# Residual tiles of both token halves kept on chip between attention and channel mixer, and the first half's token tiles made inside the second half's output projection

## The chip, the cores and the metric

The kernel runs on one core of one Trainium2 chip, as one program. The metric is the device time of one execution in microseconds (us). Tiles are 128 partitions by 512 float32 columns (256 KB) unless said otherwise.

## The reference

A decoder trunk of two layers over 1024 tokens of width 1024, float32. Layer 0 mixes tokens with two groups of eight heads (dilated window attention and forgetting attention), layer 1 with eight differential heads of value width 128. The parts that the change touches:

```python
for l in range(DEPTH):
    n = rms_norm(h, attn_norm[l])
    h = h + mixer(n)                       # heads, then concat @ w_out
    h = h + conv_glu_ffn(rms_norm(h, ffn_norm[l]), ...)
return rms_norm(h, final_norm)
```

So after the heads of a layer there are an output projection, a residual addition, a normalisation over the width, and a channel mixer (up projection to 2 x 2816, causal convolution over three tokens, SiLU gate, down projection).

## The kernel before

Activations lie transposed: the width on partitions in 8 chunks (index `m`), the tokens in columns, in two halves of 512 (`half` 0 and 1). Every product of two float32 operands is made of three matmuls on a high and a low part (`mm3`, L150; `split`, L162, writes the two parts with one ScalarE copy and one VectorE subtraction).

*Attention and its planner.* A layer's attention is a list of units (32 in layer 0, four for each pair of heads; 16 in layer 1, a head and a token half each). `weave` (L489) merges the units' steps (rows of logits, transposes, products with V, closing steps) with a list of jobs. Each step has a cost and a load; from these the planner makes a goal, the amount of job work that should be done by then, and after every step it runs job generators until the amounts that they yield reach the goal. A job with `after` waits until that unit has ended. TensorE, VectorE and ScalarE then work through queues in a fixed order that the framework's scheduler makes from this order and its own estimates. SP's and POOL's queues issue the DMAs in order: `put` (L193) is SP's, `store` (L196) POOL's.

*The jobs at a layer's end* (`out_jobs`, L1152). The heads' outputs, split, are reloaded or kept in the pool `big` (32 buffers of one tile). `job_out` (L441) then makes the output projection, a chunk `m` and a token half at a time: it asks for the base tile `rt` ahead (`fetch`), multiplies the heads' slices `ks`, and at the end `e` (L1161) adds the base to the sum in PSUM, stores the tile in DRAM (`parts`, seen as `hp` in the trace) and may add its squares to the norm's statistic (`norm_chunk`). In order:

1. heads 0 to 3, both halves, on the layer's input;
2. heads 4 to 7, first half, on the stored tile: the first half is then complete, and its statistic with it;
3. `stats`: the norm factors of the first half;
4. `blocks` (L1174): the eight tiles of the first half are loaded again from DRAM (`t`), scaled by gain and norm factor (`token_blocks`, L1118), stored in DRAM as `half0` (`nt`), and split into `nh` and `nl`, all in one step of the generator;
5. `rest`, heads 4 to 6 of the second half, on the stored tile, 24 steps of three matmuls, stored again.

Head 7 of the second half is left to the channel mixer, as its output comes last.

*Start of the channel mixer* (`channel`, L1323). The attention's buffers are given back, and the channel mixer's pool `fu` opens in their place: 16 buffers `wq`, 8 `sc`, 24 `bt`. `lead(n)` (L1037) runs the next n steps of the up projection: a weight tile is loaded (`wr`, two buffers, on SP), split (L129, L131) and multiplied with the first half's `nh` and `nl`, 12 matmuls a step, and the result goes through `sc` (L931) to DRAM (`e`). Between the leads the second half is finished: eight tiles `x` in `wq` are loaded from `parts` (L1357 to L1359), head 7 is multiplied (tag `dn`), added (L1364), squared and stored again; its statistic and factors follow. Eight tiles of the normalised first half come back from `half0` to `b0`. Then sums and differences of the two halves' blocks are formed (L1378 to L1403) and split by `cut` (L1350) into `bt`, after 24 into `big`: the up projection is a fast product of 2 x 2 blocks in seven products, whose weight sums POOL makes (L824). The down projection loads `parts` again as its residual.

Of the kernel before, what the change touches and what calls it, by code (L numbers as in the profile page):

```python
# [10 lines left out]
F32R = mybir.dt.float32r  # L11
# [7 lines left out]
P = 128  # L19
# [3 lines left out]
HT = 512  # L23
# [10 lines left out]
def f(ap):  # L34
    return ap.bitcast(F32)
# [14 lines left out]
class Trunk:  # L50
# [91 lines left out]
    last = None  # L142
# [47 lines left out]
    def small(self):  # L190
        return self.psp.tile([P, HT], F32, name="small", tag="small")
# [297 lines left out]
    def weave(self, ev, jobs, deadline, margin):  # L489

        ev.sort(key=lambda e: (e[0], e[1]))
        ftotal = sum(j.cost for j in jobs)

        C, L, c, l, first = [], [], 0.0, 0.0, {}
        for k, e in enumerate(ev):
            if e[1] == 0:
                first[e[2]] = k
            c += e[4]  # L500
            l += e[5]
            C.append(c)
            L.append(l)
        pts = [(0, 0.0)]
        for u, nj in sorted(deadline.items()):
            pts.append((first[u - margin], sum(j.cost for j in jobs[:nj])))
        pts.append((len(ev) - 1, ftotal))
        goal = [0.0] * len(ev)
        for (k0, y0), (k1, y1) in zip(pts, pts[1:]):
            dc, dl = C[k1] - C[k0], max(L[k1] - L[k0], 1e-9)  # L510
            for k in range(k0, k1 + 1):
                y = y0 + (y1 - y0 + dc) * (L[k] - L[k0]) / dl - (C[k] - C[k0])
                goal[k] = max(goal[k - 1] if k else 0.0, min(max(y, y0), y1))
        st = {"job": 0, "gen": None, "done": 0.0}
        fins = set()
        lastq = max(k for k, e in enumerate(ev) if e[1] == 1)

        def fill(upto, final=False):
            while st["done"] < upto and st["job"] < len(jobs):
                jb = jobs[st["job"]]  # L520
                if st["gen"] is None:
                    if jb.after is not None and jb.after not in fins and not final:
                        return
                    st["gen"] = jb.gen()
                try:
                    st["done"] += next(st["gen"])
                except StopIteration:
                    st["job"] += 1
                    st["gen"] = None
        for k, (tm, kind, i, fn, cost, load) in enumerate(ev):  # L530
            if kind == 0 and i in deadline:
                while st["job"] < deadline[i]:
                    fill(st["done"] + 0.1)
            if kind in self.pinned and self.last is not None:
                with self.tc.issue_after(getattr(self.last, "ins", self.last)):
                    fn()
            else:
                fn()
            if kind == 6:
                fins.add(i)  # L540
            if k == lastq:
                self.pmap["pj"] = ["A", "D", "A", "D", "D"]
            fill(goal[k])
        fill(1e9, True)
        assert st["job"] == len(jobs), (st["job"], len(jobs))
# [578 lines left out]
    def run(self):  # L1124
# [10 lines left out]
        parts = [[dr.tile([P, T], F32, name=f"hp{l}_{m}") for m in range(8)] for l in range(2)]  # L1135
# [3 lines left out]
        half0 = [dr.tile([P, HT], F32, name=f"nt{m}") for m in range(8)]  # L1139
# [8 lines left out]
        self.odirect = (6, 7)  # L1148
        cs = [slice(hf * HT, (hf + 1) * HT) for hf in range(2)]


        def out_jobs(l, w, base):  # L1152
            st, gi, O = stF[l], 2 * l + 1, Os[l]

            def add(src, norm):
                def b(m, half):
                    t = f(self.big.tile([P, HT], F32R, name="rt", tag="big"))
                    self.store(t, src(m)[:, cs[half]])
                    return t

                def e(m, half, ps, t):  # L1161
                    nc.vector.tensor_tensor(t, t, ps, ALU.add)
                    self.store(parts[l][m][:, cs[half]], t)
                    if norm:
                        self.norm_chunk(st, m, half, t, None)
                return b, e

            def stats():
                self.norm_cols(st, 0)
                yield 0.4  # L1170
                self.norm_rows(st, 0, self.ap, ("rt2", 2))
                yield 0.9

            def blocks():  # L1174
                ts = []
                for m in range(10):
                    if m < 8:
                        t = f(self.big.tile([P, HT], F32R, name="t0", tag="big"))
                        self.put(t, parts[l][m][:, cs[0]])
                        ts.append(t)  # L1180
                    if m == 0:
                        rest.fetch()
                    if 0 < m < 9:
                        self.token_blocks(st, gi, 0, m - 1, ts[m - 1])
                        self.store(half0[m - 1], ts[m - 1])
                    if m > 1:
                        hl = (self.big.tile([P, HT], F32R, name=x, tag="big") for x in ("nh", "nl"))
                        st["h"][m - 2, 0], st["l"][m - 2, 0] = hl
                        self.split(st["h"][m - 2, 0], st["l"][m - 2, 0], ts[m - 2])
                yield 0.0  # L1190
            last = lambda k: 4 * k + 3 if l == 0 else 2 * k + 1
            part = lambda m: parts[l][m]
            jobs = [self.job_load(O, k, last(k)) for k in range(4)]
            jobs += [self.job_out(w, [0, 1, 2, 3], [0, 1], O, *add(base, False), last(3))]
            jobs += [self.job_load(O, k, last(k)) for k in range(4, 6)]
            jobs += [self.job_out(w, [4, 5, 6, 7], [0], O, *add(part, True), 29 if l == 0 else 13)]
            rest = self.job_out(w, [4, 5, 6], [1], O, *add(part, False), 27 if l == 0 else 14, 3)
            jobs += [Job(stats, 1.3), Job(blocks, 0.0)]
            jobs += [rest]
            return jobs  # L1200

        def first_v(src, N):
# [3 lines left out]
        w = a["wqkA"]  # L1206
# [8 lines left out]
        for g in range(2):  # L1215
            w = a["wqkB"]
            J0 += [self.job_v(a["wvB0"], n, 4, 64, (0, 8), True) if g == 0 else
                   self.job_v(a["wvB1"], n, 4, 64, (0, 12))]
            for p in range(2 * g, 2 * g + 2):
                J0 += [self.job_plain(w[2 * p], n, -0.125, qB, p * P),  # L1220
                       self.job_plain(w[2 * p + 1], n, None, kB, p * P)]
        J0 += out_jobs(0, a["woA"], lambda m: a["xT"][m * P:(m + 1) * P, :])
        O0 = "woA7"
        F0 = self.plan_ffn(0)
# [3 lines left out]
        for g in range(4):  # L1228
            w = a["wqkC"]
            if g:  # L1230
                J1 += [self.job_v(a["wvC"][g], n, 2, P, (1, 2 * g))]
            J1 += [self.job_rope(w[4 * g], w[4 * g + 1], n, -0.125, qC, g * P),
                   self.job_rope(w[4 * g + 2], w[4 * g + 3], n, None, kC, g * P)]
        J1 += out_jobs(1, a["woC"], lambda m: hs[m])
        O1 = "woC7"
        F1 = self.plan_ffn(1)
# [12 lines left out]
        st = n = stA[0]  # L1249
# [73 lines left out]
        def channel(l, es, w7, F, after, mid):  # L1323

            st, gi = stF[l], 2 * l + 1
# [13 lines left out]
            wq = lambda: fp.tile([P, HT], F32, name="wq", tag="wq", bufs=self.nwq)  # L1339
# [4 lines left out]
            small = lambda: fp.tile([P, HT], F32R, name="bt", tag="bt", bufs=self.nbt)  # L1344
# [9 lines left out]
            lead, run = self.ffn_up(l, F, B, lambda: act(0))  # L1354
            self.wstop = F[1][1, 6] - 1
            lead(2)
            x = [wq() for _ in range(8)]  # L1357
            for m in range(8):
                self.put(x[m], parts[l][m][:, cs[1]])  # L1359
            for m in range(8):  # L1360
                ps = self.pj("dn")
                wh, wl = (t[:, m % 4 * P:(m % 4 + 1) * P] for t in o7[m // 4])
# [1 line left out]
                nc.vector.tensor_tensor(x[m], x[m], ps, ALU.add)  # L1364
                self.norm_chunk(st, m, 1, x[m], None)
                self.store(parts[l][m][:, cs[1]], x[m])
            b0 = [wq() for _ in range(4)] + [f(small()) for _ in range(4)]
            for m in (0, 4, 1, 5, 2, 6, 3, 7):
                self.put(b0[m], half0[m])
            lead(2)  # L1370
# [34 lines left out]
            h = H[l] = {}  # L1405
# [22 lines left out]
        def mid0():  # L1428
            flush()
            self.norm_cols(st1, 0)  # L1430
            self.norm_rows(st1, 0, self.fp, ("sc", self.nsc))
        es = channel(0, es, O0, F0, after0, mid0)
        flush()
        self.pmap["small"], self.pmap["gu"] = ["S"], ["A", "A", "B", "O"]
# [25 lines left out]
        for hf in range(2):  # L1460
            c = cs[hf]
            nc.vector.tensor_tensor(C[:, c], C[:, c], n["rb"][:, c], ALU.mult)
            t = ap.tile([P, HT], F32, name="rt1", tag="rt1", bufs=2)
# [26 lines left out]
        def after1(m, c):  # L1490
# [18 lines left out]
            if m == 7 and hf:  # L1509
                self.finish(acc[hf][:, o], H[1], c)  # L1510
        es = channel(1, es, O1, F1, after1, lambda: self.finish(acc[0], H[1], cs[0]))
        es.close()

# [120 lines left out]
```

## Time and profile before

| | |
|---|---|
| Median of three runs | 2571.03 us (2567.0 to 2571.26) |
| The profiled execution's own time | 2565.89 us |
| Its span, first to last instruction | 2564.1 us |
| Granted clock, mean over the span | 0.983 |
| TensorE busy, share of the span | 96% |
| VectorE / ScalarE / POOL | 77% / 48% / 28% |

Busy shares are averages over the span. TensorE's matmuls are pipelined: a 512 column matmul is shown with about 395 ns, but one follows another every 233 ns, so a busy engine is not one at its peak. The granted clock is a share of 2.4 GHz, and has two levels, 1.2 and 2.4 GHz. Time is lost on TensorE where it is idle or at the lower level.

### The profile page before, as it was taken

What the parts mean: (1) busy time and instruction counts of PE and PEld (TensorE: products, weight loads), DVE (VectorE), ACT (ScalarE), POOL (GpSimd) and SP (SyncE); (2) the same over time, 40 slices, a digit from 0 to 9 for tenths busy, and PEclk for the clock granted to TensorE, in tenths of its full rate; (3) what the DMA queues carried; (4) which work ended last, traced back from release to release, by engine and by line L of the source; (5) the groups of instructions that cost most, each with busy time, mean ns of one, the idle gap of its engine ahead of it and who ended that gap; (6) DMA issues with size and microseconds to landing.
All of it is one profiled execution on the core that took longest, in us unless ns stands there. A gap on an engine that the chain in (4) does not pass through costs nothing.

```text
span 2564.1 us, 38450 instructions
## 1 busy us (share of the span) xinstructions
PE 2467.2 (96%) x12511; PEld 2047.6 (80%) x12511; DVE 1979.0 (77%) x3885; ACT 1221.5 (48%) x2443; POOL 721.4 (28%) x978
## 2 busy tenths in 40 slices
PE   8999999998899999999999999989888999999998
PEld 7899898776688888778888888877666888887886
DVE  7778878776988988775666888878769878977656
ACT  5456655454544344454434555545454443435433
POOL 1211112222444665100021211232225456740000
PEclk9999999998999999999999999999989999999998
DMA  5655556867766887664555555696576677766644
GB/s 192 229 172 172 178 173 216 255 204 275 216 207 219 244 241 240 205 220 167 193 202 169 197 182 193 203 288 216 179 253 198 204 238 242 248 201 231 226 130 160
DMA packets 249240, 536.96 MB, mean 209 GB/s; under 512 B 37976, under 2 KB 50896, under 8 KB 249040
## 3 DMA queue, kind: packets, MB, share of 16 engines
q1 hardware_dynamic: 179792, 320.02, 39.3%
q0 software_dynamic: 68672, 213.96, 25.1%
q8 instruction: 99, 1.62, 0.3%
q14 instruction: 101, 0.83, 0.1%
q10 hardware_dynamic: 576, 0.52, 0.1%
HBM read 362.33 MB, written 172.03 MB: 208 GB/s over the span
## 4 chain that ended last, share of the span: by engine, by line
PE 79%; DVE 8%; DMA 7%; ACT 3%; issue 2%; SPq 0%; POOL 0%; DVEq 0%; ACTq 0%; POOLq 0%
PE pj L145 67%; PE D L145 5%; PE O L145 4%; PE T L148 3%; DVE wl L131 2%; DMA wr<-in_wgate 1%; DVE bt L166 1%; PE small L145 1%; DMA wr<-in_wdown 1%; ACT wh L129 1%; DVE e L590 1%; DMA ncb<-cd 1%; ACT e L739 1%; DMA wr<-in_wqkC 1%; DMA ar<-td 1%
## 5 line engine op out<-in xcount | busy, mean ns | idle before, releaser
L145 PE MATMUL pj<-bt,wh 128*128 128x512 f32 x1760 | 554.2, 395 | 13.0 <-DVE bt L166 8.6
L145 PEld LDWEIGHTS pj<-bt,wh 128*128 128x128 f32 x1760 | 331.2, 188 | 93.5 <-DVE bt L166 11.6
L131 DVE TENSOR_TENSOR wl<-wr,wh 128x512 fp32r<-128x512 f32 (+2 forms) x340 | 235.7, 696 | 180.8 <-ACT wh L129 171.1
L145 PE MATMUL pj<-nh,wh 128*128 128x512 f32 x864 | 356.9, 413 | 16.8 <-ACT nh L232 8.6
L129 ACT ACTIVATE wh<-wr 128x512 fp32r<-128x512 f32 (+2 forms) x340 | 211.4, 624 | 290.5 <-PE pj L145 122.5
L145 PE MATMUL pj<-bt,wl 128*128 128x512 f32 x880 | 347.7, 395 | 0.0
L145 PE MATMUL pj<-nl,wh 128*128 128x512 f32 x864 | 346.2, 401 | 0.0
L145 PE MATMUL pj<-nh,wl 128*128 128x512 f32 x864 | 346.0, 401 | 0.0
L131 DVE TENSOR_TENSOR wl<-wq,wh 128x512 fp32r<-128x512 f32 x268 | 278.0, 1038 | 30.4 <-ACT wh L129 30.2
L129 ACT ACTIVATE wh<-wq 128x512 fp32r<-128x512 f32 x268 | 166.7, 628 | 239.2 <-PE pj L145 186.9
L824 POOL TENSOR_TENSOR wq<-wq 128x512 f32<-128x512 f32 x132 | 195.3, 1491 | 211.4 <-DVE wl L131 102.3
L145 PE MATMUL pj<-ah,wh 128*128 128x512 f32 (+1 forms) x628 | 248.0, 396 | 2.5 <-ACT s L1086 1.2
L145 PE MATMUL pj<-ah,wl 128*128 128x512 f32 (+1 forms) x628 | 246.2, 393 | 0.0
L145 PE MATMUL pj<-al,wh 128*128 128x512 f32 (+1 forms) x628 | 246.1, 392 | 0.0
L145 PEld LDWEIGHTS pj<-nh,wh 128*128 128x128 f32 x864 | 166.1, 192 | 49.9 <-ACT nh L232 8.6
L165 ACT ACTIVATE ph<-T 128x512 fp32r<-128x512 f32 (+3 forms) x288 | 138.9, 486 | 131.5 <-PE T L148 128.7
L145 PEld LDWEIGHTS pj<-bt,wl 128*128 128x128 f32 x880 | 165.8, 188 | 39.0
L145 PEld LDWEIGHTS pj<-nh,wl 128*128 128x128 f32 x864 | 165.5, 192 | 37.9 <-DVE wl L131 0.4
L145 PEld LDWEIGHTS pj<-nl,wh 128*128 128x128 f32 x864 | 166.2, 192 | 31.1 <-DVE nl L247 0.5
L166 DVE TENSOR_TENSOR pl<-T,ph 128x512 fp32r<-128x512 f32 (+3 forms) x288 | 157.5, 552 | 34.2 <-ACT ph L165 32.9
L148 PE MATMUL T<-ident,e 128*128 128x128 f32 x864 | 144.1, 277 | 19.2 <-DVE e L746 13.5
L145 PE MATMUL pj<-wh,nh 128*128 128x256 f32 (+1 forms) x512 | 149.0, 293 | 0.0
(476 smaller groups left out, 5339.7 us busy)
## 6 DMA issues: line engine op xcount, KB each, us to landing
wq<-in_wgate SPq DMA_DIRECT2D x88, 256.0 KB, 3.7
wq<-in_wup SPq DMA_DIRECT2D x88, 256.0 KB, 3.9
act<-v POOLq DMA_DIRECT2D x44, 512.0 KB, 3.6
td<-sc POOLq DMA_DIRECT2D x80, 256.0 KB, 4.5
wq<-in_wdown SPq DMA_DIRECT2D x80, 256.0 KB, 4.4
sd<-wq POOLq DMA_DIRECT2D x80, 256.0 KB, 4.1
ar<-td SPq DMA_DIRECT2D x80, 256.0 KB, 3.8
wr<-sd SPq DMA_DIRECT2D x80, 256.0 KB, 3.8
```

Of the source, the lines that this page charges most:

```text
L129: nc.scalar.activation(hi[:, :n], raw[:, :n], AF.Copy)
L131: nc.vector.tensor_tensor(lo[:, :n], raw[:, :n], f(hi[:, :n]), ALU.subtract)
L145: self.last = self.nc.tensor.matmul(*args, **kw)
L148: self.last = self.nc.tensor.transpose(*args)
L165: nc.scalar.activation(hi, src, AF.Copy)
L166: nc.vector.tensor_tensor(lo, src, f(hi), ALU.subtract)
L590: self.nc.vector.tensor_tensor_reduce(out=e[:, k0:k0 + w], in0=d[:, :w], in1=in1(k0, w), scale=1.0, scalar=init, op0=ALU.add, op1=ALU.min, ...
L739: nc.scalar.activation(e[m][:, :W], e[m][:, :W], AF.Exp, scale=-1.0, bias=nm[:, m:m + 1], accum_out=ls[:, m, i4:i4 + 1])
L824: nc.gpsimd.tensor_tensor(dst, x, y, op)
```

## The change

The half-0 tile that `e` completes is kept (`t0`) and no longer loaded again, though still stored. The half-1 tile that `rest` completes is kept as well (`t1`), not stored, and the channel mixer takes it in place of a load. `blocks` takes over the job `rest`: after each token tile it runs up to three steps of `rest` if the unit that `rest` waits for has ended (27 in layer 0, 14 in layer 1), and else yields 0.1 three times. `b0` lies wholly in `wq`.

```diff
             def add(src, keep=None):
...
                 def e(m, half, ps, t):
                     nc.vector.tensor_tensor(t, t, ps, ALU.add)
-                    self.store(parts[l][m][:, cs[half]], t)
-                    if norm:
-                        self.norm_chunk(st, m, half, t, None)
+                    if half == 0 or keep is None:
+                        self.store(parts[l][m][:, cs[half]], t)
+                    if keep is not None:
+                        keep[m] = t
+                        if half == 0:
+                            self.norm_chunk(st, m, half, t, None)
...
             def blocks():
-                ts = []
-                for m in range(10):
+                rest.fetch()
+                more = rest.gen()
+                for m in range(9):
                     if m < 8:
-                        t = f(self.big.tile([P, HT], F32R, name="t0", tag="big"))
-                        self.put(t, parts[l][m][:, cs[0]])
-                        ts.append(t)
-                    if m == 0:
-                        rest.fetch()
-                    if 0 < m < 9:
-                        self.token_blocks(st, gi, 0, m - 1, ts[m - 1])
-                        self.store(half0[m - 1], ts[m - 1])
-                    if m > 1:
+                        self.token_blocks(st, gi, 0, m, t0[m])
+                        self.store(half0[m], t0[m])
+                    if m > 0:
                         hl = (self.big.tile([P, HT], F32R, name=x, tag="big") for x in ("nh", "nl"))
-                        st["h"][m - 2, 0], st["l"][m - 2, 0] = hl
-                        self.split(st["h"][m - 2, 0], st["l"][m - 2, 0], ts[m - 2])
-                yield 0.0
+                        st["h"][m - 1, 0], st["l"][m - 1, 0] = hl
+                        self.split(st["h"][m - 1, 0], st["l"][m - 1, 0], t0[m - 1])
+                    for _ in range(3):
+                        yield next(more, 0.0) if rest.after in self.fins else 0.1
+                while rest.after not in self.fins:
+                    yield 0.1
+                yield from more
+            t0, self.t1[l] = {}, {}
...
-            jobs += [self.job_out(w, [4, 5, 6, 7], [0], O, *add(part, True), 29 if l == 0 else 13)]
-            rest = self.job_out(w, [4, 5, 6], [1], O, *add(part, False), 27 if l == 0 else 14, 3)
-            jobs += [Job(stats, 1.3), Job(blocks, 0.0)]
-            jobs += [rest]
+            jobs += [self.job_out(w, [4, 5, 6, 7], [0], O, *add(part, t0), 29 if l == 0 else 13)]
+            rest = self.job_out(w, [4, 5, 6], [1], O, *add(part, self.t1[l]), 27 if l == 0 else 14, 3)
+            jobs += [Job(stats, 1.3), Job(blocks, rest.cost)]
...
-            x = [wq() for _ in range(8)]
-            for m in range(8):
-                self.put(x[m], parts[l][m][:, cs[1]])
+            x = [self.t1[l][m] for m in range(8)]
...
-            b0 = [wq() for _ in range(4)] + [f(small()) for _ in range(4)]
+            b0 = [wq() for _ in range(8)]
```

## Rows read from the trace of the kernel before

**Rows 1.** The page: busy time of each engine over the span.

```profile
PE 2467.2 (96%) x12511; PEld 2047.6 (80%) x12511; DVE 1979.0 (77%) x3885; ACT 1221.5 (48%) x2443; POOL 721.4 (28%) x978
```

**Rows 2.** Busy time by stage: stretch, width, engines (instructions), clock, DMA share, GB/s.

```profile
570.00:614.00 44.00, 40.37 (x196) 32.88 (x197) 33.00 (x72) 19.56 (x38) 11.33 (x21) 0.84 0.62 206
614.00:645.00 31.00, 26.39 (x105) 20.39 (x104) 16.44 (x35) 13.07 (x24) 7.07 (x14) 0.89 0.89 321
645.00:700.00 55.00, 47.19 (x189) 36.23 (x188) 54.42 (x63) 30.25 (x54) 27.73 (x29) 0.94 0.74 223
1819.00:1835.00 16.00, 8.65 (x44) 6.12 (x43) 15.78 (x34) 9.32 (x24) 5.93 (x11) 0.85 0.50 184
1835.00:1870.00 35.00, 28.87 (x133) 22.51 (x131) 18.54 (x42) 12.34 (x31) 5.40 (x10) 0.92 0.45 151
1870.00:1905.00 35.00, 27.51 (x100) 20.91 (x101) 19.07 (x37) 15.85 (x28) 9.94 (x17) 0.85 0.92 330
1905.00:1980.00 75.00, 67.24 (x278) 53.18 (x277) 70.59 (x85) 35.76 (x65) 37.04 (x36) 0.95 0.62 193
```

**Rows 3.** DMA issues of the whole span: queue, count, KB each, median us to landing.

```profile
hp<-rt POOLq DMA_DIRECT2D x64, 256.0 KB, 3.7
...
rt<-hp POOLq DMA_DIRECT2D x32, 256.0 KB, 5.9
...
t<-hp SPq DMA_DIRECT2D x16, 256.0 KB, 5.5
nt<-t POOLq DMA_DIRECT2D x16, 256.0 KB, 2.6
wq<-hp SPq DMA_DIRECT2D x16, 256.0 KB, 6.5
```

**Rows 4.** Tile t, layer 0: the token tiles' operations, min/median/max ns.

```profile
L1120 DVE SCALAR_TENSOR_TENSOR t<-t,gn,rb x8: 741/744/752, 579.2 to 590.3; 128x512 f32<-128x512 f32 x8
...
L166 DVE TENSOR_TENSOR nl<-t,nh x8: 679/682/691, 581.2 to 592.9; 128x512 fp32r<-128x512 f32 x8
```

**Rows 5.** Timeline of TensorE, layer 0: start, duration, line, operation [idle before, releaser].

```profile
590.47 0.50 PE L145 MATMUL D<-KS,QS 128*128 128x512 f32 x1 [2.05 <-DVE mn L590]
...
592.37 0.77 PE L145 MATMUL pj<-oh__7079,wh 128*128 128x512 f32 x1 [1.09 <-DVE st L590]
...
620.04 0.50 PE L145 MATMUL pj<-oh__7929,o 128*128 128x512 f32 x1 [1.49 <-DVE wq L1364]
...
631.35 0.50 PE L145 MATMUL pj<-nh,wh 128*128 128x512 f32 x1 [2.62 <-ACT sc L931]
```

**Rows 6.** The same columns as rows 2, ten microseconds of layer 0.

```profile
590.00:600.00 10.00, 8.44 (x27) 6.50 (x28) 9.19 (x21) 3.24 (x6) 5.37 (x10) 0.66 0.80 243
```

**Rows 7.** Chain of waits: start, duration, what, in the channel mixer of layer 0.

```profile
690.73 363.71 PE pj L145 x1562
```

**Rows 8.** Timeline of TensorE, layer 1.

```profile
1831.30 0.87 PE L148 MATMUL T<-ident,e 128*128 128x128 f32 x3 [4.46 <-DVE e L746]
...
1861.43 1.12 PE L148 MATMUL small<-ident,Ra 128*128 128x128 f32 x4 [3.48 <-ACT Ra L759]
...
1870.11 0.51 PE L145 MATMUL pj<-oh__20973,o 128*128 128x512 f32 x1 [1.11 <-ACT o L165]
...
1880.15 0.50 PE L145 MATMUL pj<-oh__20973,o 128*128 128x512 f32 x1 [2.18 <-DVE wq L1364]
```

**Rows 9.** Timeline of ScalarE, layer 1.

```profile
1855.81 0.63 ACT L129 ACTIVATE wh<-wr 128x512 fp32r<-128x512 f32 x1 [4.72 <-DMA wr<-in_wgate]
...
1860.80 0.58 ACT L759 ACTIVATE Ra<-O 128x512 f32<-128x512 f32 x1
...
1895.17 1.28 ACT L129 ACTIVATE wh<-wr 128x512 fp32r<-128x512 f32 x2 [4.19 <-DMA wr<-in_wgate]
```

**Rows 10.** Timeline of SP's DMA queue, layer 1.

```profile
1872.13 4.91 SPq L194 DMA_DIRECT2D wq<-hp  x7
...
1883.99 1.02 SPq L127 DMA_DIRECT2D wr<-in_wgate  x2
```

More of the change, by code (lines that the diff above doesn't have):

```diff
@@ L514, in weave @@
         st = {"job": 0, "gen": None, "done": 0.0}
-        fins = set()
+        fins = self.fins = set()
         lastq = max(k for k, e in enumerate(ev) if e[1] == 1)
@@ L1149, in run, with add @@
         cs = [slice(hf * HT, (hf + 1) * HT) for hf in range(2)]
+        self.t1 = {}
         def out_jobs(l, w, base):
             st, gi, O = stF[l], 2 * l + 1, Os[l]
-            def add(src, norm):
+            def add(src, keep=None):
                 def b(m, half):
@@ L1193, in out_jobs @@
             jobs = [self.job_load(O, k, last(k)) for k in range(4)]
-            jobs += [self.job_out(w, [0, 1, 2, 3], [0, 1], O, *add(base, False), last(3))]
+            jobs += [self.job_out(w, [0, 1, 2, 3], [0, 1], O, *add(base), last(3))]
             jobs += [self.job_load(O, k, last(k)) for k in range(4, 6)]
-            jobs += [self.job_out(w, [4, 5, 6, 7], [0], O, *add(part, True), 29 if l == 0 else 13)]
-            rest = self.job_out(w, [4, 5, 6], [1], O, *add(part, False), 27 if l == 0 else 14, 3)
-            jobs += [Job(stats, 1.3), Job(blocks, 0.0)]
-            jobs += [rest]
+            jobs += [self.job_out(w, [4, 5, 6, 7], [0], O, *add(part, t0), 29 if l == 0 else 13)]
+            rest = self.job_out(w, [4, 5, 6], [1], O, *add(part, self.t1[l]), 27 if l == 0 else 14, 3)
+            jobs += [Job(stats, 1.3), Job(blocks, rest.cost)]
             return jobs
```

## Prediction

> **What bounds the kernel now.** I read the page's engine totals first. TensorE is busy 2467.2 of 2564.1 us, VectorE 1979.0 [rows 1]. The change takes no arithmetic from either, so it can only win stalls, and I looked for these where the changed code stands: from the end of each layer's attention to the start of its channel mixer. Cut into stages [rows 2], these stretches show what TensorE loses. I count as loss the width less the busy time, plus one less the granted clock, times the width (a stretch at half of the 2.4 GHz does half the columns):
>
> A, 570 to 614, end of layer 0's weave: 3.6 + 7.0 = 10.7 us. B, 614 to 645, start of its channel mixer: 4.6 + 3.4 = 8.0. C, 645 to 700: 7.8 + 3.3 = 11.1. D, 1819 to 1835, layer 1's token tiles: 7.4 + 2.4 = 9.8. E, 1835 to 1870, its last unit: 6.1 + 2.8 = 8.9. F, 1870 to 1905, start of its channel mixer: 7.5 + 5.3 = 12.7. G, 1905 to 1980: 7.8 + 3.8 = 11.5.
>
> Some 73 us in all. In C and G VectorE is busy 54.4 of 55 and 70.6 of 75 us: it is the bound there. In B and F it is busy about half, but the DMA engines are at 0.89 and 0.92 of their time: there the loads bound.
>
> **The change part by part.**
>
> *DMAs that go.* Per layer, eight reloads of half-0 tiles `t` (SP's queue), eight stores of the second half (POOL's), and eight reloads into `wq` (SP's): 48 transfers of 256 KB in both layers [rows 3], 12.6 MB. The 16 stores of `hp<-rt` that go were half 1; half 0 is still stored, since the down projection reads it back.
>
> *Term 1, layer 0's token tiles spread out.* Each tile costs VectorE a scaling of 0.744 and a subtraction of 0.682 us [rows 4], eight of them 11.4 us. Before, the eight are handed out at one point; TensorE then waits 2.05 us for a row minimum and 1.09 us for a row statistic on VectorE [rows 5], and in the ten us from 590 the granted clock is 0.66 [rows 6], that is 6.8 us at 1.2 GHz, worth 3.4 us. I worked through the planner's arithmetic for this layer: the 24 matmul steps of heads 4 to 6 keep their places, and tokens 0 to 7 come ahead of steps 0, 3, 6, ..., 21. Each is now covered by nine matmuls, 9 x 0.233 = 2.1 us (0.233 is 363.71 us over 1562 matmuls [rows 7]). POOL's queue changes too: the loads `rt<-hp`, which stood behind all eight `nt<-t`, are now asked for first. Worth 0 to 6.5 us; I take 4, as VectorE has 11 us spare in A [rows 2], but its work must still be done.
>
> *Term 2, no reload of the second half in layer 0.* The additions after the output projection of head 7 wait on SP's eight loads, with a median landing of 6.5 us [rows 3]. TensorE waits 1.49 us for the first addition's bank and 2.62 us for a copy that stands on ScalarE's queue behind the squares of these additions [rows 5]. Without the loads the next eight (`nt`) and the weights behind them move up on SP by some 6 us. Worth 0 to the whole 8.0 of B; I take 5.
>
> *Term 3, layer 1's token tiles.* Here the planner does not spread them. The second job waits for unit 14 (head 6, second half); until then the new generator yields 0.1 three times per tile. By the planner's sums the first tile comes at goal 249.27, and the next event raises the goal to 252.33: all others are made at once. The burst moves behind one row of the last unit and remains. Its wait of 4.46 us [rows 8] may shrink or grow: 0, bounds -3 and +3.
>
> *Term 4, order at layer 1's end.* The 0.1's go on eating the plan: when unit 14 ends, 262.68 of 264.34 are used, so 3 of the 24 steps come with the last unit and 21 after it. Before, 22 stood ahead of the last unit's last transpose. Now the last unit's tail goes first, and the output projection hides its chain. Before, ScalarE's copy `Ra` started at 1860.80, behind a weight copy that waited 4.72 us for its DMA [rows 9]; TensorE waited 3.48 us for it, and 1.11 us at 1870.11 [rows 8]. Eight stores `hp<-rt` no longer run beside these weight loads. Worth 0 to the 8.9 of E; I take 5.
>
> *Term 5, no reload in layer 1.* SP issues seven of the eight reloads from 1872.13 for 4.91 us, and its next weight only at 1883.99 [rows 10]; that weight lands at 1895.17, where ScalarE had waited 4.19 us [rows 9]. TensorE waits 2.18 us for an addition [rows 8], and the clock is 0.85 over F [rows 2]. Worth 0 to 12.7; I take 7. Here the Trainium skill has a rule, in DMA: Bandwidth & Descriptors, section Issuing engines are not separate DMA queues: DMAs from all queues run on the same 16 engines and interleave. By that rule the stores that leave POOL's queue also speed SP's weights; were the queues separate, term 4 would keep only its change of order, an estimated 3 us, and the sum would fall by 2. The 0.92 of F with both queues at work speaks for the rule.
>
> *Term 6, the stages behind.* C and G are VectorE's. If they only start earlier with the same inside, they win nothing more; if TensorE's lead tiles last longer because VectorE's chain started sooner, up to half of their 22.6 us. The second normalised half now takes eight `wq` buffers instead of four, but the residual eight are gone, so four more are free for raw weights. I take 3, bounds 0 and 11.
>
> *Term 7, what is new.* The 21 steps behind the last unit are 63 matmuls, 14.7 us. They hide the chain from `Ra` to head 7's output (1860.80 to 1870.11, 9.3 us [rows 8, 9]); if none of them ran earlier in gaps, 5.4 us stand bare. I take 3, bounds 0 and 5.4. Arithmetic, splits and additions are the same in number: 0, on the engines that did them before.
>
> **The sum.** 4 + 5 + 0 + 5 + 7 + 3 - 3 = 21 us. Against the profiled execution (span 2564.1, its own time 2565.9 us) that gives 2544.9; the median of the runs is 5.1 us above that execution, so I put it at 2571.0 - 21 = 2550.
>
> **The rivals.**
>
> *More: the waits fall whole.* Terms 2, 4 and 5 at their upper ends (8.0 + 8.9 + 12.7), term 1 at 6.5, term 6 at 8, term 7 at 3: 41 us, 2530. For it: all stalls of B and F follow late loads. Against it: other loads stay on SP (eight `nt`, weights).
>
> *No change: VectorE gives it back.* From 614 to 700 it is busy 70.9 of 86 us and from 1905 to 1980 94%; if the last tile of C and G is due when it was, earlier starts vanish there: 0 to 4 us left, 2567 to 2571. For it: C and G lose about as much as B and F together, with VectorE as the bound. Against it: their first work needs the additions of B and F. The Trainium skill's Perfetto Trace Analysis, section Identifying the Most-Contended Engine, says to optimise the engine with the highest occupancy first (for DMA by HBM utilisation). By that rule the change misses the bound: it takes no instruction from TensorE, and 2571 stays. TensorE's 96% of the span speaks for it, its losses in B and F against it.
>
> *Slower: the pool of 32 tiles runs full.* Layer 0, at token m: 6 output tiles of heads 4 to 6, 8 - m of the first half left, 2m splits, m + 3 of the second half: 17 + 2m and those not yet released. At m = 6 that is 29, at 7 (with all eight of the second half) 29, then 32 with head 7. Layer 1 ends at 16 + 8 + 8 = 32 too. Each `rt` load that must wait for a store `nt` (2.6) and then land itself (5.9 [rows 3]) takes 8.5 us where its steps take 2.1. It decides once tokens are released three or more behind in layer 0, and one tile late in layer 1. Three loads in each layer are 6 x 6.4 = 38 us against 21 won: 17 us slower, 2588. Against it: stores land in 2.6 us, hardly more than one token's 2.1.
>
> **How the numbers follow.** Forecast 0.57, more 0.14, no change 0.16, slower 0.13. 0.2% (5.1 us) is about what a measurement of this kernel can tell from no change. Faster: the forecast, the greater gain and a small part of the no-change case, 0.75; same 0.13; slower 0.12. The bounds reach from 50 us won to 17 lost; leaving out a tenth on each side gives 2532 to 2571; the forecast's own range is 2540 to 2562.
>
> **What would show it.** In the trace after: no `wq<-hp` and no `t<-hp`; the scalings in layer 0 about 2 to 3 us apart instead of 11 us together; still together in layer 1; the copy `Ra` of the last unit within 2 us of its last matmul; the first addition of head 7 under 2 us behind its matmuls; the weight that follows `nt` on SP issued some 6 us sooner after head 7's output; losses in B and F halved. Wrong would be: a second half tile's load or a split waiting for a release, C and G longer by what B and F lost, or TensorE without work while the 21 steps wait for additions.

## The result, and the profile after

The changed kernel takes 2540.27 us (median of four runs, 2534.91 to 2545.66) against 2571.15 us beside it (four runs, 2567.0 to 2576.09): a ratio of 0.9879, 95% interval 0.9852 to 0.9907, 30.9 us less. The forecast was 2550, 21 us less. The profiled execution took 2534.91 us, its span is 2533.1 us.

The page's totals, with the columns of [rows 1]:

```profile
PE 2449.5 (97%) x12511; PEld 2038.7 (80%) x12511; DVE 1970.6 (78%) x3885; ACT 1220.3 (48%) x2443; POOL 720.8 (28%) x962
```

TensorE, VectorE and ScalarE have exactly as many instructions as before [rows 1]; POOL has 16 fewer, the stores. What was won is stall. The stages of [rows 2] again, with the same columns, each cut at the event that ended it before: A ends just ahead of head 7's first matmul, B with layer 0's second norm factors, and so on.

```profile
569.00:603.40 34.40, 32.73 (x186) 27.01 (x184) 31.05 (x64) 17.95 (x35) 7.03 (x13) 1.00 0.45 151
603.40:631.00 27.60, 23.56 (x95) 18.60 (x96) 16.84 (x35) 13.89 (x27) 8.52 (x15) 0.88 0.89 319
631.00:688.00 57.00, 49.01 (x194) 38.47 (x193) 54.53 (x67) 29.32 (x53) 33.44 (x28) 0.91 0.65 202
1804.00:1820.00 16.00, 8.42 (x44) 6.95 (x44) 15.72 (x35) 9.79 (x25) 7.01 (x13) 0.79 0.47 165
1820.00:1849.00 29.00, 27.10 (x142) 21.56 (x141) 20.44 (x47) 13.25 (x31) 0.55 (x1) 1.00 0.42 142
1849.00:1878.00 29.00, 23.41 (x96) 17.60 (x95) 20.68 (x33) 13.29 (x24) 13.79 (x19) 0.92 0.97 319
1878.00:1951.00 73.00, 70.03 (x294) 55.60 (x293) 67.30 (x91) 38.68 (x69) 33.80 (x34) 0.98 0.61 191
```

Loss counted as in the prediction:

| stage | before | after | won |
|---|---|---|---|
| A, end of layer 0's weave | 10.7 | 1.7 | 9.0 |
| B, start of its channel mixer | 8.0 | 7.4 | 0.6 |
| C, behind it | 11.1 | 13.1 | -2.0 |
| D, layer 1's token tiles | 9.8 | 10.9 | -1.1 |
| E, its last unit | 8.9 | 1.9 | 7.0 |
| F, start of its channel mixer | 12.7 | 7.9 | 4.8 |
| G, behind it | 11.5 | 4.4 | 7.1 |

Together 25.4 of the 31 us between the two spans. Another 3.2 us come from a stage that the prediction did not look at, ahead of D: layer 1 starts 10.8 us sooner than before, yet the products `O` of its last unit but one, at 1809.72 before, start at 1795.76, 14.0 us sooner. The likely reason is that of half of A, below: SP's queue waited 7.2 us in three landings of `hp<-rt` there too, and after the change in none.

What the prediction named as its marks. The DMA issues that answer to [rows 3], with the same columns; `t<-hp` and `wq<-hp` are gone, and `hp<-rt` is still 64, since head 7's 16 stores now leave from an `rt` tile:

```profile
hp<-rt POOLq DMA_DIRECT2D x64, 256.0 KB, 4.2
rt<-hp POOLq DMA_DIRECT2D x32, 256.0 KB, 5.2
...
nt<-rt POOLq DMA_DIRECT2D x16, 256.0 KB, 2.5
wq<-nt SPq DMA_DIRECT2D x16, 256.0 KB, 5.8
```

The scalings of the token tiles, layer 0 and layer 1 (the last times are those of the first and the last start):

```profile
L1120 DVE SCALAR_TENSOR_TENSOR rt<-rt,gn,rb x8: 733/743/752, 572.7 to 594.9; 128x512 f32<-128x512 f32 x8
...
L1120 DVE SCALAR_TENSOR_TENSOR rt<-rt,gn,rb x8: 747/748/750, 1805.7 to 1813.4; 128x512 f32<-128x512 f32 x8
```

In layer 0 they are spread over 22 us in place of 11 [rows 4], in layer 1 they are a burst still, as predicted. Waits of TensorE that are left around the change, and ScalarE's copy of the last unit:

```profile
604.33 0.79 PE L145 MATMUL pj<-oh__7905,o 128*128 128x512 f32 x1 [2.58 <-ACT o L165]
...
618.99 0.50 PE L145 MATMUL pj<-nh,wh 128*128 128x512 f32 x1 [1.92 <-ACT sc L931]
...
1815.41 1.11 PE L148 MATMUL small<-ident,Ra 128*128 128x128 f32 x4 [7.58 <-DVE pl L166]
...
1854.44 0.50 PE L145 MATMUL pj<-oh__20779,o 128*128 128x512 f32 x1 [1.31 <-DVE rt L1366]
1858.44 0.50 PE L145 MATMUL pj<-oh__20779,o 128*128 128x512 f32 x1 [1.88 <-DVE rt L1366]
```

```profile
1831.40 0.58 ACT L759 ACTIVATE Ra<-O 128x512 f32<-128x512 f32 x1
...
1846.82 0.63 ACT L165 ACTIVATE o<-wr 128x512 fp32r<-128x512 f32 x1 [3.01 <-DMA wr<-in_woC]
```

`Ra` comes right behind the last product `O` (1831.07 for 0.27 us), and no matmul waits for it; before, the wait was 3.48 us [rows 8]. The largest wait left is the burst's, 7.58 us at 1815.41.

**What was not foreseen: SP's queue in the weave.** The queue of SP in the kernel before, layer 0 (start, duration of the issue or of the row of issues, line, transfer):

```profile
546.17 1.01 SPq L127 DMA_DIRECT2D wr<-in_woA  x2
550.68 0.33 SPq L194 DMA_DIRECT2D t<-hp  x1
551.81 0.33 SPq L127 DMA_DIRECT2D wr<-in_woA  x1
553.15 0.33 SPq L194 DMA_DIRECT2D t<-hp  x1
554.69 0.33 SPq L127 DMA_DIRECT2D wr<-in_woA  x1
558.35 0.33 SPq L194 DMA_DIRECT2D t<-hp  x1
560.95 17.10 SPq L127 DMA_DIRECT2D wr<-in_woA  x5
```

and what this queue waited for, 535 to 600 (us in total, times, the longest):

```profile
SPq L194 <- DMA hp<-rt: 7.7, 3, 3.4
```

A reload of a token tile may start only when the store of that tile has landed. Three of them stand between output weights, so SP waits 7.7 us, and with it every weight queued behind. ScalarE, which splits these weights, waits for them, first before, then after:

```profile
559.80 0.53 ACT L129 ACTIVATE wh<-wr 128x384 fp32r<-128x384 f32 x1 [3.78 <-DMA wr<-in_woA]
563.53 0.53 ACT L129 ACTIVATE wh<-wr 128x384 fp32r<-128x384 f32 x1 [2.69 <-DMA wr<-in_woA]
```

```profile
555.33 0.53 ACT L129 ACTIVATE wh<-wr 128x384 fp32r<-128x384 f32 x1 [0.41 <-DMA wr<-in_woA]
559.10 0.53 ACT L129 ACTIVATE wh<-wr 128x384 fp32r<-128x384 f32 x1 [2.71 <-DMA wr<-in_woA]
```

SP's queue after, and TensorE's stretches (columns of [rows 2]), first before, then after:

```profile
545.07 27.65 SPq L127 DMA_DIRECT2D wr<-in_woA  x9
```

```profile
560.00:570.00 10.00, 7.77 (x42) 5.95 (x40) 7.84 (x14) 5.06 (x10) 1.62 (x3) 1.00 0.54 199
570.00:580.00 10.00, 9.76 (x42) 8.18 (x43) 5.21 (x20) 3.13 (x8) 0.54 (x1) 0.66 0.27 94
```

```profile
560.00:570.00 10.00, 9.67 (x57) 7.98 (x57) 7.55 (x19) 4.97 (x12) 1.09 (x2) 1.00 0.38 131
570.00:580.00 10.00, 9.98 (x59) 8.15 (x58) 9.64 (x22) 4.88 (x10) 2.84 (x6) 1.00 0.47 157
```

Before, TensorE lost 2.2 us from 560 and then 3.4 us at the lower clock (0.66 of ten us); after, 0.4 us in both.

### The profile page after: what moved, and what is told of

The parts are those of the page before. It is cut to its first block, busy times and chain, and to the rows that moved or that the text cites. A ratio compares the mean times of both kernels' runs of the same rounds, so it can differ in the third digit from the quotient of the medians.

```text
span 2533.1 us, 38327 instructions
## 1 busy us (share of the span) xinstructions
PE 2449.5 (97%) x12511; PEld 2038.7 (80%) x12511; DVE 1970.6 (78%) x3885; ACT 1220.3 (48%) x2443; POOL 720.8 (28%) x962
## 4 chain that ended last, share of the span: by engine, by line
PE 79%; DMA 7%; DVE 6%; issue 4%; ACT 2%; POOL 0%; SPq 0%; DVEq 0%; ACTq 0%; POOLq 0%
PE pj L145 66%; PE D L145 5%; PE O L145 4%; PE T L148 4%; DMA wr<-in_wgate 2%; DVE wl L131 2%; DMA wr<-in_wdown 1%; PE small L145 1%; ACT wh L129 1%; DMA ncb<-cd 1%; DMA ar<-td 1%; DVE e L590 1%; ACT e L739 1%; DMA wr<-in_woC 0%; DMA ar<-act 0%
## 5 line engine op out<-in xcount | busy, mean ns | idle before, releaser
L824 POOL TENSOR_TENSOR wq<-wq 128x512 f32<-128x512 f32 x132 | 203.8, 1549 | 204.8 <-DVE wl L131 100.6
```

The lines of the kernel that those rows point to most:

```text
L824: nc.gpsimd.tensor_tensor(dst, x, y, op)
```

## The experiments

Medians are of all runs of a kernel, ratios are to the kernel before, run beside it on the same chip; an interval is about 0.2 to 0.4% wide, so two kernels whose ratios differ by less than some 0.2% are not told apart here.

**First half kept, nothing else.** Layer order as before; the second half goes through DRAM as before.

```diff
-                    if m < 8:
-                        t = f(self.big.tile([P, HT], F32R, name="t0", tag="big"))
-                        self.put(t, parts[l][m][:, cs[0]])
-                        ts.append(t)
...
-                        self.token_blocks(st, gi, 0, m - 1, ts[m - 1])
+                        self.token_blocks(st, gi, 0, m, t0[m])
```

> The kernel before with one part of the change: the first half's eight tiles are kept and not loaded again; all eight token tiles are still made at once, and the second half is stored and loaded again as before. Theory queue: SP's reloads of tiles that had just been stored held the weights behind them (in the kernel before three reloads on SP waited 7.7 us in all for their stores in layer 0 and 7.2 us in layer 1), so keeping the tiles alone brings 8 to 13 us: some 6 to 9 in layer 0 before head 7's first matmul and some 3 in layer 1. Theory spread: what layer 0 won comes from the token tiles' new places, so this run is within 3 us of the kernel before.

2562.77 us against 2570.87, ratio 0.9968 (0.9957 to 0.9979): 8.1 us won. SP issues its nine weights in one row (27.63 us from 544.85), head 7's first matmul of layer 0 comes at 610.46 in place of 614.96. The burst is still there: from 580 to 590 TensorE is busy 7.86 us at 0.67. The 8.1 us are the medians' figure; the trace, of the slowest of the seven executions (2566.05 us), does not hold them to its end. Layer 0's second norm factors come 6.3 us sooner than before (638.26 against 644.54), but layer 1's first copy `Ra` only 0.3 sooner (1394.60 against 1394.86): in this execution the channel mixer in between gives the gain back.

**Second half kept, nothing else.**

```diff
-                    self.store(parts[l][m][:, cs[half]], t)
+                    if keep is None:
+                        self.store(parts[l][m][:, cs[half]], t)
+                    else:
+                        keep[m] = t
...
-            x = [wq() for _ in range(8)]
-            for m in range(8):
-                self.put(x[m], parts[l][m][:, cs[1]])
+            x = [self.t1[l][m] for m in range(8)]
...
-            b0 = [wq() for _ in range(4)] + [f(small()) for _ in range(4)]
+            b0 = [wq() for _ in range(8)]
```

> The kernel before with the other part: the second half's tiles stay on chip, neither stored after heads 4 to 6 nor loaded again by the channel mixer; the order of the work is that of before, and the first half is loaded again. Terms 2 and 5 of the prediction give 12 us, with the share of term 4 that came from the stores 14 us: 10 to 15 us faster than before. Rival, that what layer 1 won between 1835 and 1905 us came from the new order: 3 to 6 us, nearly all of it in layer 0.

2554.29 us, ratio 0.994 (0.9926 to 0.9954): 16.6 us won. Three loads `t<-hp` still stand between SP's weights and wait 6.9 us, yet from 570 to 580 TensorE is busy 9.99 us at clock 1.00. In layer 1 the wait for `Ra` falls from 3.48 to 0.76 us though the order is the old one. POOL asks for all five base tiles of that stretch between 1825.30 and 1827.96; before, the last two, at 1848.01 and 1851.32, stood behind stores `hp<-rt`, the first of which had waited 13.17 us for its addition.

**Both kept, order of before.** The changed kernel with the token tiles in one step and `rest` behind them as a job of its own:

```diff
-                    for _ in range(3):
-                        yield next(more, 0.0) if rest.after in self.fins else 0.1
-                while rest.after not in self.fins:
-                    yield 0.1
-                yield from more
+                yield 0.0
...
-            jobs += [Job(stats, 1.3), Job(blocks, rest.cost)]
+            jobs += [Job(stats, 1.3), Job(blocks, 0.0), rest]
```

> Both halves kept, but the order of before: all eight token tiles at once, then heads 4 to 6 of the second half as a job of its own. If keeping explains the gain, 22 to 28 us faster than before, 3 to 9 us slower than the changed kernel. If the new order explains it (spread tiles in layer 0, the last unit's tail ahead of the 21 steps in layer 1), at least 12 us slower than the changed kernel.

2548.42 us, ratio 0.9911 (0.9898 to 0.9924): 22.5 us won, nearly the sum of the two alone (8.1 + 16.6 = 24.7).

**The new order in layer 0 alone.** The same edit as the last, for `l == 1` only.

> The changed kernel, but in layer 1 the order of before (tokens at once, then the 24 steps right behind unit 14). Term 4 right (the last unit's tail first is worth 3 to 8 us): 3 to 8 us slower than the changed kernel, with the last unit's copy to Ra again behind weight copies on ScalarE. Rival, term 7 (the 21 steps behind the last unit stand bare): as fast or up to 5 us faster.

2543.07 us, ratio 0.9898 (0.9884 to 0.9912): 5.4 us below the last kernel on the same chip, though the intervals overlap, so the size is not firm. The trace agrees up to the channel mixer: layer 0's second norm factors come at 630.6 in place of 638.7, and from 580 to 590 TensorE is busy 10.00 us at clock 1.00. But layer 1's first copy `Ra` comes only 0.8 us sooner (1386.40 against 1387.18), so how the 5.4 us reach the end is not shown.

**The changed kernel again**, beside the next three.

> The changed kernel itself, as the measure for the three kernels that run beside it on the same chip. Every theory: 0.988 of before, about 2540 us.

2543.41 us, ratio 0.9889 (0.9874 to 0.9904). Against the kernel with layer 1's old order this is no difference: the new order in layer 1 wins nothing that can be measured, which leaves room for some 5 us either way.

**Layer 1's token tiles spread.**

```diff
-                        yield next(more, 0.0) if rest.after in self.fins else 0.1
+                        yield next(more, 0.0) if rest.after in self.fins else 0.55
```

> The changed kernel, but while unit 14 has not ended, each of the three yields after a token tile is 0.55 instead of 0.1 of the plan, so that layer 1's eight token tiles no longer come at one point. Theory A (the burst costs its stall): TensorE's wait of 7.58 us at 1815.41 and the low clock from 1810 to 1820 (0.66, 3.4 us) fall; VectorE's 11 us must still be done in that unit, so 3 to 8 us of the 11 come back: 0.997 to 0.9985 of the changed kernel. Rival B (VectorE bounds the last unit): it is busy 9.7 of 10 us there with or without the burst, the wait only moves: within 2 us of the changed kernel. Rival C: the token tiles come later and the channel mixer's first split waits for them: slower by 2 to 6 us.

2540.76 us, ratio 0.988 (0.9861 to 0.9898); not told apart from the changed kernel. The tiles are spread, and the wait has moved with them (the scalings, then TensorE's timeline):

```profile
L1120 DVE SCALAR_TENSOR_TENSOR rt<-rt,gn,rb x8: 730/749/751, 1811.0 to 1826.9; 128x512 f32<-128x512 f32 x8
```

```profile
1820.00 0.90 PE L148 MATMUL T<-ident,e 128*128 128x128 f32 x3 [3.11 <-DVE pl L166]
```

From 1800 to 1832 the loss is 9.3 us against 11.7 in the changed kernel run beside it, with VectorE busy 29.6 of 32 us. The time and VectorE's share are what rival B expects: VectorE bounds this unit, however the tiles are dealt out.

**Head 7's weights first.** SP loads no weight of the up projection ahead of head 7's output weights.

```diff
             jobs += [Job(stats, 1.3), Job(blocks, rest.cost)]
+            self.rstop[l] = len(self.wq) - 1
...
+        self.wstop = self.rstop[0]
         self.weave(self.events(units, dict(cl=3.0, ct=2.0, cp=3.4)), J0[1:],
...
+        self.wstop = self.rstop[1]
```

> The changed kernel, but no up projection weight is loaded on SP's queue ahead of head 7's own output weights. Theory A (what is left at the channel mixer's start hangs on those weights): TensorE's 2.58 us at 604.33 go, and in layer 1 head 7's first matmul comes some 6 us earlier than 1849.2, since its output is ready at about 1840.7 and its weights' split starts at 1846.82; the tiles behind it come earlier by as much: 3 to 8 us won, 0.997 to 0.999 of the changed kernel. Rival B (lead tiles fill the wait): the up projection's own weights come later by what head 7's come sooner, TensorE is idle for them instead: within 2 us, or slower by up to 4 us.

2552.07 us, ratio 0.9924 (0.9904 to 0.9945), by the medians 8.7 us slower than the changed kernel beside it, more than either theory gave. Its six runs spread from 2543.96 to 2562.82 us, and the profiled one (2546.52) is only 3.6 us above the repeat's, so the size is uncertain. Two rows, the columns of [rows 2] and TensorE's timeline:

```profile
590.00:600.00 10.00, 6.48 (x47) 5.30 (x45) 8.01 (x14) 4.23 (x8) 1.08 (x2) 0.98 0.16 59
```

```profile
624.66 0.79 PE L145 MATMUL pj<-nh,wh 128*128 128x512 f32 x1 [4.05 <-ACT sc L931]
```

Head 7's first matmul of layer 0 is 4.2 us sooner (600.89 against 605.09), but its last is not (614.43 against 614.04): the up projection's steps had filled TensorE under the last unit's tail, and without their weights it is busy 6.48 of ten us from 590 on (10.00 in the repeat). The wait of 2.58 us that was to go is there as before, and it was never one for weights. In the changed kernel ScalarE splits head 7's output and right behind it the weights, without a wait for their DMA:

```profile
603.13 0.63 ACT L165 ACTIVATE oh__7905<-o 128x512 fp32r<-128x512 f32 x1 [0.75 <-DVE o L699]
603.67 1.13 ACT L165 ACTIVATE o<-wr 128x512 fp32r<-128x512 f32 x2
```

What TensorE waits for is the last unit's own chain, from its last product at 601.53 through ScalarE and VectorE to these splits. The chain stands bare because of the new order in layer 0: with both halves kept and the old order head 7's first matmul (609.56) has no such wait, with the new order in layer 0 alone (603.90) it has the same 2.58 us.

**The reloads on POOL's queue.** The kernel before, no byte fewer:

```diff
-                        self.put(t, parts[l][m][:, cs[0]])
+                        self.store(t, parts[l][m][:, cs[0]])
```

> The kernel before, with the eight reloads of the first half's tiles in each layer issued on POOL's queue instead of SP's; no transfer is left out. Keeping these tiles on chip and nothing else had won 8 us. Theory A (SP's queue stands): a reload on SP must wait for its tile's store to land, and the output weights queued behind it on SP wait with it, so moving the reloads to POOL's queue wins 4 to 8 us without saving a byte: 0.997 to 0.9985 of before. Rival B (the bytes count): the 4 MB are moved all the same, and the result is within 2 us of before. Rival C: the reloads hold up what follows on POOL's queue (base tiles, stores of the normalised tiles): slower by 2 to 8 us.

2569.48 us, ratio 0.9995 (0.9983 to 1.0007): nothing won. Theory A's half can be seen, SP's nine weights in one row (27.64 us from 545.11) and TensorE busy 9.66 and 9.98 of ten us from 560 and 570 at full clock. But POOL's queue takes over the wait (POOL's issues, then TensorE):

```profile
588.65 0.54 POOL L197 DMA_DIRECT2D nt<-t  x1 [2.36 <-DVE t L1120]
589.91 0.54 POOL L197 DMA_DIRECT2D nt<-t  x1 [0.72 <-DVE t L1120]
590.44 2.71 POOL L197 DMA_DIRECT2D rt<-hp  x5
```

```profile
592.62 1.54 PE L148 MATMUL T<-ident,e 128*128 128x128 f32 x6 [4.16 <-DVE pl L166]
596.29 0.80 PE L145 MATMUL pj<-oh__7079,wh 128*128 128x512 f32 x1 [2.12 <-DVE rt L1162]
```

The burst starts when the reloads land, its stores stand ahead of five base tiles `rt`, and TensorE waits 4.16 us behind the burst and 2.12 us for an addition to a late base tile. So SP's queue alone is not the price of 8 us: the wait is real, but a reload has to stand in some queue, and here each queue has something urgent behind it. Rival B forecast the same time, that the bytes count; against it speaks the run below in which the same bytes move again at no cost that shows, though in another order.

**The second half's tiles still stored.** The changed kernel with the stores of `rest` left in:

```diff
-                    if half == 0 or keep is None:
-                        self.store(parts[l][m][:, cs[half]], t)
+                    self.store(parts[l][m][:, cs[half]], t)
```

> The changed kernel, but the second half's tiles that heads 4 to 6 complete are still stored to DRAM (8 stores of 256 KB a layer), though nothing loads them; they are stored once more after head 7 as before. Theory A (the reloads held up the queues, the stores did not): within 2 us of the changed kernel, 0.987 to 0.990 of before. Rival B (the stores' bytes slow the weights beside them, as the DMA share of 0.9 to 1.0 behind the last unit lets one think): 3 to 6 us slower than the changed kernel.

2549.0 us (2547.6 to 2550.22), ratio 0.9916 (0.9899 to 0.9933): 5.6 to 8.7 us above the changed kernel's two medians, and each of its five runs above every run of the three kernels beside it (the next three). Rival B's size, but not for its reason. In layer 0 nothing is lost (second norm factors at 632.2, as in the changed kernel's repeat); in layer 1 head 7's first matmul comes at 1859.49 in place of 1850.08. POOL's issues there, and TensorE's longest wait:

```profile
1835.35 0.54 POOL L197 DMA_DIRECT2D hp<-rt  x1 [17.21 <-DVE rt L1164]
1836.41 0.54 POOL L197 DMA_DIRECT2D hp<-rt  x1 [0.53 <-DVE rt L1164]
1837.48 0.54 POOL L197 DMA_DIRECT2D hp<-rt  x1 [0.53 <-DVE rt L1164]
1838.01 2.66 POOL L197 DMA_DIRECT2D rt<-hp  x5
```

```profile
1851.61 0.77 PE L145 MATMUL pj<-nh,wh 128*128 128x512 f32 x1 [5.71 <-DVE rt L1164]
```

Five base tiles stand behind three stores, which wait for additions behind the last unit. In the repeat of the changed kernel the last base tile is asked for at 1819.57. From 1832 to 1850 the DMA engines' share is 0.53, the same as in that repeat: not bytes, but the place in a queue.

**First half reloaded, in the new order.** The changed kernel, each token tile loaded again on SP where it is scaled:

```diff
                     if m < 8:
+                        t0[m] = f(self.big.tile([P, HT], F32R, name="t0", tag="big"))
+                        self.put(t0[m], parts[l][m][:, cs[0]])
                         self.token_blocks(st, gi, 0, m, t0[m])
```

> The changed kernel, but each token tile of the first half is loaded again from DRAM on SP's queue where it is scaled; the second half stays on chip and the order is the changed one. Theory A (the reloads are dear in any order, since what is queued behind them waits): 5 to 9 us slower than the changed kernel, and SP's row of nine output weights in layer 0 is broken up again. Rival B (they are dear only in one burst): spread over the steps they are covered, within 3 us of the changed kernel.

2543.99 us, ratio 0.9892 (0.9872 to 0.9912): within what can be told from the changed kernel, rival B. SP's nine weights are broken up (3, 1 and 5), but SP no longer waits for a landing of `hp<-rt`: six of the eight reloads of layer 0 are issued after 574, when their stores have long landed. The 8 us of the first experiment are thus not the price of reloads as such. Whether it is their place right behind the stores or the single step that makes them dear, these runs do not separate. In this trace layer 1's second norm factors come 6.0 us later than in the repeat (1886.74 against 1880.79), and what follows takes 655.0 us against 660.3: the same time is not the same course.

**Block loads four steps later**, and **the same with layer 1's tiles spread**:

```diff
-            for m in (0, 4, 1, 5, 2, 6, 3, 7):
-                self.put(b0[m], half0[m])
             lead(2)
             self.norm_cols(st, 1)
             lead(2)
+            for m in (0, 4, 1, 5, 2, 6, 3, 7):
+                self.put(b0[m], half0[m])
```

> The changed kernel, but the eight loads of the normalised first half into wq are asked for four up projection steps later, behind the weights of these steps. Theory A (at the channel mixer's start these loads, now free to go at once, compete with the weights: DMA share 0.93 to 1.02 from 1850 to 1870, and VectorE's additions stand behind splits that wait for a weight): the waits of 1.2 to 2.2 us on additions and on ScalarE's copy go, 3 to 6 us won over both layers. Rival B (the bytes are the same and are only moved): the wait comes back where the blocks are first used, within 2 us or slower by up to 5 us.

> The kernel with the later block loads, and layer 1's token tiles spread as in the earlier run with 0.55. If both gains stand and add: 2 us below the better of the two alone, 0.985 to 0.987 of before. If the stages that follow are bound by VectorE and take up what is won: the same as the changed kernel, within 2 us.

2541.36 us, ratio 0.9888 (0.9871 to 0.9905), and 2539.69 us, ratio 0.9877 (0.9859 to 0.9895). Neither is told apart from the changed kernel. From head 7's first matmul to the second norm factors layer 1 takes 30.9 us with the later loads (1847.69 to 1878.6) and 30.7 without (1850.08 to 1880.8), and from 1850 to 1870 the DMA engines' share is 0.99: the loads are moved, and the DMA engines are as full as before (0.97 in the repeat). No version of these beats the change by a difference that shows.

## Why the prediction was right, and where it was not

The account by kernels: first half kept 8.1 us, second half kept as well 14.4 (2562.77 to 2548.42), new order in layer 0 5.4, at the edge of what can be told, new order in layer 1 nothing; 27.8 of the 30.9 us, and the repeat of the changed kernel has 28.0. The forecast's direction held, and its mechanism, stalls behind transfers and VectorE's burst, held in the main; it was 9.7 us too high, for one missing term above all. That the result still lies at the lower end of the forecast's range is in part luck: the missing term was worth some 8 us, and term 2 was too large by more than 4 the other way.

- **"DMAs that go": the step that failed.** The loads `t` were counted and priced at nothing. Taking them alone out of the kernel before is worth 8.1 us. The prediction had [rows 3] with `t<-hp` on SP's queue, but looked at SP's queue only in layer 1's channel mixer [rows 10], not in the weave, where a load waited for the store just ahead of it. A's loss was put down to VectorE's burst alone.
- **Term 1** (4 us): 5.4 measured by the kernels with and without the new order in layer 0. That agrees, at the edge of what can be told; so does its sign that the scalings spread and the clock from 590 stays up. The new order has a price that the term left out: the last unit's chain in layer 0 stands bare for 2.58 us. A as a whole won 9.0: the burst and the reloads.
- **Term 2** (5 us): too large. B's loss fell by 0.6 us and its width from 31 to 27.6. The eight loads `wq<-nt` took the place of the eight that went (SP issues them from 605.00 on), and the DMA engines' share stays at 0.89. "The next eight move up" was right, and they meet the same weights. The sign "losses in B and F halved" did not come: 7.4 of 8.0 and 7.9 of 12.7 us are left.
- **Term 3** (0): right; D lost 10.9 us in place of 9.8, with a wait of 7.58 in place of 4.46 us [rows 8].
- **Terms 4, 5 and 7** (5 + 7 - 3 = 9 us): E and F won 11.8. The sum was nearly right, and one reason not borne out: the order of layer 1's end, credited in term 4, wins nothing that can be measured. It frees `Ra`, but in the old order without the stores the wait for `Ra` is down to 1.06 us as well (the kernel with layer 1's old order), and the time is the same. With the stores, the new order would have cost 6 to 9 us in POOL's queue. Term 4's other reason, the stores gone from beside the weights, holds, though through the queue's order. Term 7's bare wait did not come: E loses 1.9 us in 29.
- **Term 6** (3 us): 5.1, G 7.1 and C -2.0.
- **The rivals.** "VectorE gives it back" is what C shows in layer 0 (VectorE busy 54.5 of 57 us, nothing won), but not G; two traces above show it too: the 6.3 us of the first half kept, and the 8.1 of the new order in layer 0, are 0.3 and 0.8 us by layer 1's first copy `Ra`. By the Trainium skill's Perfetto Trace Analysis, section Identifying the Most-Contended Engine, the engine of highest occupancy is optimised first, and TensorE is judged by the arithmetic it does against its peak and by the busy share of its weight loads, not by that of its matmuls. The prediction took the matmuls' 96%; the weight loads have 80% [rows 1], ahead of VectorE's 77%, so the rule names TensorE by these too. It does not say that 2571 stays, as the prediction had it: the change took no instruction from TensorE, and 31 us of its waits and low clock went. "The pool runs full": in the changed stretches the base tiles `rt` on POOL's queue wait once, 1.3 us for a DMA that is not a store `nt`; the 7.58 us of D are VectorE's.
- The rule that term 5 drew on is not what the stores' price shows: that price came at an unchanged DMA share. Whether it played a part in F, where the share is 0.97, no run here separates.

Left open: which share of the second half's 14.4 us lies with the loads and which with the stores in the old order; the stores were put back in the new order only. The two traces give a hint for layer 1: with the second half kept, the wait behind its burst ends 8.7 us sooner than before (1822.64 against 1831.30), head 7's first matmul, ahead of which no load of that half stands, 12.8 sooner (1857.28 against 1870.11), and the second norm factors 20.0 sooner (1884.49 against 1904.50): some 4 us without the loads, some 7 beside them.

## What to carry to other kernels

Before pricing a DMA by its bytes, write out the queue that issues it, in order, over the whole stretch: a load that needs a store just made holds all that is queued behind it, and moving it to another queue only changes what it holds. The reloads in one step, three of them right behind their stores, were worth 8 us, and spread in the new order, six of the eight some 20 us behind their stores, nothing that shows. A reorder is to be judged together with the transfers that it carries along: with the stores left in, layer 1's new order cost 6 to 9 us. Before a wait is put down to a transfer, look at what the operation that ends it waited for itself.

## What the runs showed of the hardware that was not expected

- SP's queue stood 7.7 us in three waits for landings of stores of 256 KB. TensorE lost 2.2 us from 560 to 570, and from 570 to 580 its granted clock was 0.66, worth 3.4 us more. With the second half kept the same three waits came to 6.9 us, TensorE lost 1.6 us from 560 to 570, and the clock stayed at 1.00: the clock's part does not follow from the queue's wait alone, and what decides it is not shown here.
- Without the up projection's weights ahead of head 7's own, TensorE was busy 6.48 of ten us from 590 to 600, in place of 10.00, and the median was 8.7 us higher, in runs that spread widely.
